# Late modulation in a hybrid diffusion block: w_ada tiles loaded one step ahead, multiplied and added on GpSimd instead of VectorE

## The chip, the cores and the metric

The kernel runs on one core of a Trainium2 chip. The metric is device time in microseconds (us): the median of three runs was 1921.36 us before the change (1921.07 to 1922.86). The engines are named as the profile names them: PE is TensorE's matmuls and PEld its weight loads, DVE is VectorE, ACT is ScalarE, POOL is GpSimd, SP is the engine whose queue issues all the loads.

## The reference

One layer of a block with three parallel token mixers, 256 latent tokens and 256 context tokens of width 2048, all in float32. What is computed, cut to what matters here:

```python
sh_m, sc_m, g_m, sh_f, sc_f, g_f = split(silu(c) @ w_ada + b_ada, 6)   # w_ada: 2048 x 12288
hl = rmsnorm(x) * (1 + sc_m) + sh_m          # and the same for the context
p  = hl @ w_in                               # 2048 x 13376: SSD x, B, C, dt; z; pool; Fourier; gates
y_ssd, y_pool, y_four = ...                  # bidirectional Mamba-2 scan, box pooling, 2-D DFT
merged = g0 * y_pool + g1 * y_four + g2 * y_ssd
x = x + g_m * (merged @ w_out)
x = x + g_f * swiglu(rmsnorm(x) * (1 + sc_f) + sh_f)                    # 2048 -> 5632 -> 2048
return rmsnorm(x) * final_norm_w
```

The first two of the six modulation vectors, `sh_m` and `sc_m`, are needed before the first projection. The other four, 2048 columns of `w_ada` each, are needed later: `sc_f`, `sh_f` and `g_m` around the output projection, `g_f` at the first down projection. These four are the late modulation.

## The kernel before

Every large product is made three times over to keep float32 accuracy: a weight tile `raw` (128 partitions x 1024 numbers, 512 KB) is split into an upper part `whi` by a cast on ACT (`S.copy`, L124) and a lower part `wlo` by a subtraction on DVE (`V.tensor_tensor`, L125), and PE makes upper x upper, lower x upper and upper x lower (`mm3`, L143 to L145). `stage` (L132) does the load and the split; `proj` (L595) goes through a matrix in steps of one `raw` tile, twelve 512-column matmuls for each step. `raw` has four buffers, `whi` and `wlo` three each (pool `wp`).

All loads are issued by one queue, SP. Its order is the order of the program text where the first part is written by hand; behind that, `load` (L95) ties each further load behind the last weight load. So SP issues loads one after another, and each waits until the buffer that it fills has been released. The other engines' order is made by a scheduler from the order of the program text and fixed in the program; each engine works through its own list in that order.

The late modulation is `ada_rest` (L344), a generator. A unit of it is one tile of `w_ada` of 128 rows and 1024 columns: it is loaded into a `raw` buffer, and DVE adds it, times silu(c) of its rows (`sil`, one number per partition), to the accumulator `adacc`: `tensor_scalar` (L353) for the first of sixteen units, `scalar_tensor_tensor` (L355) for the other fifteen. After sixteen units `adacc` is split like a weight, and small matmuls sum over its partitions (`strip` or `ones_r`). There are 8 such sums, 128 units in all. `bg` (L392) makes units behind the steps of the products: the table `BG` says how many units go with each step, 0.5 for the letters x, u, z (and the columns C), 0.35 for p, F, f, q, and 0.45 for s, the first five gate and up products of the SwiGLU. The first 96 units run behind the projections of the mixer; 32 units (`g_f`) run behind the SwiGLU's first products.

In the SSD (`ssd`, L493) ACT and DVE make small matrices `rh` (tag "R", `QR` buffers) that PE turns into decays.

Of the kernel before, what the change touches and what calls it, by code (L numbers as in the profile page):

```python
# [11 lines left out]
F32 = mybir.dt.float32  # L12
F32R = mybir.dt.float32r
AF = mybir.ActivationFunctionType
ALU = mybir.AluOpType

P = 128
D = 2048
KT = D // P
# [17 lines left out]
CH = 512  # L37
# [29 lines left out]

QR, QE = 4, 1
APART, APART2, TURNS0, TURNS1 = 3, 3, 1, 1
ORDER = "u P x0 c x1 u s0 x2 s1 z0 F x3 P z1 s2 p0 F z2 p1 f0 s3 z3 p2 f1 Y f2 p3 q0 f3 q1 q2 q3"  # L70
BG = {"x": 0.5, "z": 0.5, "u": 0.5, "p": 0.35, "F": 0.35, "f": 0.35, "q": 0.35, "s": 0.45}


@with_exitstack
def hybrid_block(ctx: ExitStack, tc, io):
# [24 lines left out]
    def nm(s):  # L100
        names[0] += 1
        return f"{s}{names[0]}"
# [24 lines left out]
    def stage_raw(src, n=CH):  # L127
        raw = wp.tile([P, 2, n], F32, tag="raw", name=nm("raw"), bufs=4)
        last[0] = nc.sync.dma_start(raw, src)
        return raw  # L130
# [15 lines left out]

    # ---------------------------------------------------------------- constants
    pp = C([P, PP_N], nme="pp")
# [40 lines left out]

    # ---------------------------------------------------------------- input norms  # L190
    xnT = [H([P, 2, CH], nme="xnT") for _ in range(8)]
# [37 lines left out]

    # ---------------------------------------------------------------- modulation of the mixer, B and dt  # L230
    Am = C([P, KT, 2], nme="Am")
# [58 lines left out]
    def project_bc(b):  # L290
        """B, dt and the first columns of x of quantum b, in steps"""
        hi, lo = stage(None, CH, w_raw[b][0])
        xhi, xlo = stage(None, 256, w_raw[b][1])
        yield

        def part(out, h, l, cs):
            for k in range(2):
                kt = 2 * b + k
                mm3(out, h[:, k, cs], l[:, k, cs], hh[b][:, k, :], hl[b][:, k, :], kt == 0, kt == KT - 1)

        for ct in range(4):
            part(bacc_[ct], hi, lo, slice(ct * P, (ct + 1) * P))
            yield
        for k in range(2):
            kt = 2 * b + k
            w = dtp[kt // 8][:, kt % 8, :]
            T.matmul(dtps, w, hh[b][:, k, :], start=kt == 0, stop=False)
            T.matmul(dtps, w, hl[b][:, k, :], start=False, stop=kt == KT - 1)
        yield
        for ct in range(2):  # L310
            part(xacc0[ct], xhi, xlo, slice(ct * P, (ct + 1) * P))
            yield
# [4 lines left out]
    nc.sync.dma_start(dtw, rows(w_in, 0, KT, DT_OFF, 64))  # L317
    # the parts of the columns of dt side by side: upper, lower
    dtp = [H([P, 8, P], F32R, nme="dtp") for _ in range(2)]
# [16 lines left out]

    # ---------------------------------------------------------------- background: rest of the modulation
    Af = C([P, KT], nme="Af")
# [4 lines left out]

    def ada_rest(offs):  # L344
        for off in offs:
            for half in range(2):
                a = wp.tile([P, 1024], F32, tag="adacc", name=nm("adacc"), bufs=1)
                for kt in range(KT):
                    raw = wp.tile([P, 1024], F32, tag="raw", name=nm("raw"), bufs=4)
                    c0 = off + half * 1024  # L350
                    load(raw, w_ada[kt * P : (kt + 1) * P, c0 : c0 + 1024])
                    if kt == 0:
                        V.tensor_scalar(a, raw, sil[:, kt : kt + 1], None, ALU.mult)  # L353
                    else:
                        V.scalar_tensor_tensor(a, raw, sil[:, kt : kt + 1], a, ALU.mult, ALU.add)  # L355
                    yield
# [40 lines left out]

    # ---------------------------------------------------------------- convolution
    def conv(dst, src, ct, ns):
        """dst, src: (P, ns, 256); depthwise taps of channel tile ct, then silu."""  # L400
        o = Q([P, ns, 256], nme="cv")
        w = [cwh[:, 5 * ct + k : 5 * ct + k + 1] for k in range(5)]
        S.activation(o, src, AF.Identity, bias=cwh[:, 120 + ct : 121 + ct], scale=w[2])
        for k in (1, 3, 0, 4):
            d = k - 2
            a, b = max(0, -d), 256 - max(0, d)
            V.scalar_tensor_tensor(o[:, :, a:b], src[:, :, a + d : b + d], w[k], o[:, :, a:b], ALU.mult, ALU.add)  # L407
        t = Q([P, ns, 256], nme="cvt")
        S.activation(t, o, AF.Tanh)
        V.scalar_tensor_tensor(dst, t, 1.0, o, ALU.add, ALU.mult)  # L410
# [7 lines left out]

    # ---------------------------------------------------------------- dt, decays
    def cs(ap):  # L420
# [56 lines left out]

    # ---------------------------------------------------------------- B, C
    BT = [H([P, 2, 2, 256], nme="BT") for _ in range(2)]
# [3 lines left out]

    # ---------------------------------------------------------------- SSD
    def bh(ap, n):
# [101 lines left out]

    # ---------------------------------------------------------------- token-major projections
    def h_op(kt, t):
# [154 lines left out]

    # ---------------------------------------------------------------- pooling
    dh, dl = [], []
# [25 lines left out]

    # ---------------------------------------------------------------- Fourier
    tabs = []
# [56 lines left out]

    # ---------------------------------------------------------------- output projection, residual
    def to_feature(chunks, scale=None, colscale=None):
        """(P, 2, CH) token-major chunks to split feature-major (P, 4, 256) tiles."""
        oh, ol = [], []
# [34 lines left out]
    def norm_ffn(t):  # L870
        """scales the rows of token tile t; returns four functions that turn and modulate them"""
        if t == 0:
# [37 lines left out]

    # the last columns and the first of the next product: the norm of one token tile under the products of the other
    def stage_h(w, p, c0):
        raw = wp.tile([P, 2, CH], F32, tag="raw", name=nm("raw"), bufs=4)
        hi, lo = H([P, 2, CH], F32R, nme="hhi"), H([P, 2, CH], F32R, nme="hlo")
        last[0] = nc.sync.dma_start(raw, rows(w, 2 * p, 2, c0, CH))
        split(hi, lo, raw)
        return hi, lo
# [50 lines left out]

    # ---------------------------------------------------------------- SwiGLU
    ah, al = [None] * NFC, [None] * NFC  # L970
# [33 lines left out]

    def down(n0, n1):
        for n in range(4):
            ps = proj(io["w_ffn_down"], 4 * n0, 4 * (n1 - n0), n * CH, pair_op(ah[n0:n1], al[n0:n1]))
            for t in range(2):
                add_down(ps[t], n, t)
# [9 lines left out]
    for n in range(4):  # L1019
        for p in range(2):  # L1020
            raw = wp.tile([P, 2, CH], F32, tag="raw", name=nm("raw"), bufs=4)
            hi, lo = H([P, 2, CH], F32R, nme="dhi"), H([P, 2, CH], F32R, nme="dlo")
# [118 lines left out]
```

## Time and profile before

| | before |
|---|---|
| median of three runs | 1921.36 us (1921.07 to 1922.86) |
| span of the profiled execution | 1922.6 us |
| PE, DVE, ACT, POOL busy | 96%, 64%, 44%, 0% of the span |
| mean granted PE clock | 0.990 |
| bytes moved by DMA | 409.19 MB, mean 213 GB/s |

The profiled execution has no time of its own beside its span, which goes from the first to the last instruction; the span lies inside the range of the three runs, so nothing of weight lies around it. PE's busy share counts a matmul from its start to its modelled end, and these overlap: matmuls of 512 columns start every 0.23 us and are shown as 0.39 us long. A PE that waits shorter than that overlap still reads as busy.

Within the span: the input norms and the early modulation take the first 156 us, the projections of the mixer go to about 1012 us, the output projection to about 1165 us, and then come the SwiGLU's products, of which the first 235 us have the units of `g_f` behind them.

### The profile page before, as it was taken

What the parts mean: (1) busy time and instruction counts of PE and PEld (TensorE: products, weight loads), DVE (VectorE), ACT (ScalarE), POOL (GpSimd) and SP (SyncE); (2) the same over time, 40 slices, a digit from 0 to 9 for tenths busy, and PEclk for the clock granted to TensorE, in tenths of its full rate; (3) what the DMA queues carried; (4) which work ended last, traced back from release to release, by engine and by line L of the source; (5) the groups of instructions that cost most, each with busy time, mean ns of one, the idle gap of its engine ahead of it and who ended that gap; (6) DMA issues with size and microseconds to landing.
All of it is one profiled execution on the core that took longest, in us unless ns stands there. A gap on an engine that the chain in (4) does not pass through costs nothing.

```text
span 1922.6 us, 23276 instructions
## 1 busy us (share of the span) xinstructions
PE 1847.1 (96%) x8804; PEld 1483.4 (77%) x8804; DVE 1236.8 (64%) x1515; ACT 852.5 (44%) x1177; POOL 0.2 (0%) x4
## 2 busy tenths in 40 slices
PE   5999999999999999999999999999999999999998
PEld 3677886867777768777877887787788888888886
DVE  4338869695886687766656657666655555555567
ACT  5225535464464454533434544443343444433444
POOL 0000000000000000000000000000000000000000
PEclk8999999999999999999999999999999999999999
DMA  9985745454656747677777665787766666656655
GB/s 333 353 288 158 243 145 167 142 155 158 186 157 208 248 152 252 216 250 247 244 248 245 201 226 152 256 277 260 247 211 191 196 188 186 191 192 196 187 186 175
DMA packets 214081, 409.19 MB, mean 213 GB/s; under 512 B 14801, under 2 KB 51793, under 8 KB 213969
## 3 DMA queue, kind: packets, MB, share of 16 engines
q1 hardware_dynamic: 213968, 407.71, 67.1%
q8 instruction: 69, 1.13, 0.3%
q14 instruction: 44, 0.35, 0.1%
HBM read 405.56 MB, written 2.10 MB: 212 GB/s over the span
## 4 chain that ended last, share of the span: by engine, by line
PE 66%; DMA 17%; DVE 11%; issue 4%; ACT 2%; DVEq 0%; SPq 0%; ACTq 0%
PE acc L144 19%; PE acc L145 19%; PE acc L143 19%; DMA raw<-w_ada 14%; DVE wlo L125 5%; DVE adacc L355 2%; PE aux L262 1%; DVE cv L407 1%; PE aux L560 1%; DMA t<-ptab 1%; PE aux L522 1%; DMA raw<-w_in 1%; ACT whi L124 1%; PE aux L759 1%; DMA psc<-pool_scale 1%
## 5 line engine op out<-in xcount | busy, mean ns | idle before, releaser
L124 ACT CAST whi<-raw 128x1024 fp32r<-128x1024 f32 (+1 forms) x553 | 574.2, 1040 | 799.5 <-PE acc L145 554.2
L125 DVE TENSOR_TENSOR wlo<-raw,whi 128x1024 fp32r<-128x1024 f32 (+1 forms) x553 | 662.3, 1207 | 354.2 <-ACT whi L124 353.3
L144 PE MATMUL acc<-wlo,h2h 128*128 128x512 f32 x704 | 275.4, 391 | 2.5 <-DVE wlo L125 2.5
L143 PE MATMUL acc<-whi,h2h 128*128 128x512 f32 x704 | 275.0, 391 | 2.3 <-ACT h2h L124 2.3
L145 PE MATMUL acc<-whi,h2l 128*128 128x512 f32 x704 | 275.4, 391 | 0.0
L355 DVE SCALAR_TENSOR_TENSOR adacc<-raw,sil,adacc 128x1024 f32<-128x1024 f32 x120 | 154.0, 1283 | 176.1 <-DMA raw<-w_ada 175.8
L144 PE MATMUL acc<-wlo,lh 128*128 128x512 f32 x512 | 201.8, 394 | 5.4 <-DVE wlo L125 5.4
L143 PE MATMUL acc<-whi,lh 128*128 128x512 f32 x512 | 201.3, 393 | 0.0
L145 PE MATMUL acc<-whi,ll 128*128 128x512 f32 x512 | 200.6, 392 | 0.0
L144 PEld LDWEIGHTS acc<-wlo,h2h 128*128 128x128 f32 x704 | 132.4, 188 | 30.9 <-DVE wlo L125 3.8
L143 PEld LDWEIGHTS acc<-whi,h2h 128*128 128x128 f32 x704 | 132.3, 188 | 29.6 <-ACT h2h L124 2.7
L145 PEld LDWEIGHTS acc<-whi,h2l 128*128 128x128 f32 x704 | 132.5, 188 | 28.2 <-DVE h2l L125 1.3
L145 PE MATMUL acc<-whi,al 128*128 128x512 f32 x320 | 124.7, 390 | 0.0
L144 PE MATMUL acc<-wlo,ah 128*128 128x512 f32 x320 | 124.7, 390 | 0.0
L143 PE MATMUL acc<-whi,ah 128*128 128x512 f32 x320 | 124.6, 389 | 0.0
L144 PEld LDWEIGHTS acc<-wlo,lh 128*128 128x128 f32 x512 | 96.1, 188 | 29.9 <-DVE wlo L125 9.9
L145 PE MATMUL acc<-hh,wlo 128*128 128x512 f32 x288 | 113.8, 396 | 0.8 <-DVE wlo L125 0.8
L144 PE MATMUL acc<-hl,whi 128*128 128x512 f32 x288 | 114.5, 398 | 0.0
L143 PE MATMUL acc<-hh,whi 128*128 128x512 f32 x288 | 112.1, 402 | 0.9 <-ACT whi L124 0.9
L143 PEld LDWEIGHTS acc<-whi,lh 128*128 128x128 f32 x512 | 96.1, 188 | 20.7 <-issue 0.8
L145 PEld LDWEIGHTS acc<-whi,ll 128*128 128x128 f32 x512 | 96.1, 188 | 19.8 <-issue 0.2
L145 PEld LDWEIGHTS acc<-whi,al 128*128 128x128 f32 x320 | 60.1, 188 | 12.4
(294 smaller groups left out, 2467.8 us busy)
## 6 DMA issues: line engine op xcount, KB each, us to landing
raw<-w_in SPq DMA_DIRECT2D x200, 512.0 KB, 4.6
raw<-w_ada SPq DMA_DIRECT2D x192, 512.0 KB, 5.1
raw<-w_ffn_gate SPq DMA_DIRECT2D x88, 512.0 KB, 4.4
raw<-w_ffn_up SPq DMA_DIRECT2D x88, 512.0 KB, 4.4
raw<-w_ffn_down SPq DMA_DIRECT2D x88, 512.0 KB, 4.1
raw<-w_ssd_out SPq DMA_DIRECT2D x32, 512.0 KB, 4.9
raw<-w_out SPq DMA_DIRECT2D x32, 512.0 KB, 4.2
raw<-w_fourier SPq DMA_DIRECT2D x16, 512.0 KB, 4.5
```

The costliest lines, as they stand in the source:

```text
L124: S.copy(hi, src)
L125: V.tensor_tensor(lo, src, hi.bitcast(F32), ALU.subtract)
L143: T.matmul(out, ah, bh, start=first, stop=False)
L144: T.matmul(out, ah, bl, start=False, stop=False)
L145: T.matmul(out, al, bh, start=False, stop=last)
L262: T.matmul(ps[32 * k : 32 * k + 32, o], stat[:, 4 * p + k, :], raws[8 * j + i][:, k, :], start=p == 0, stop=p == 3)
L355: V.scalar_tensor_tensor(a, raw, sil[:, kt : kt + 1], a, ALU.mult, ALU.add)
L407: V.scalar_tensor_tensor(o[:, :, a:b], src[:, :, a + d : b + d], w[k], o[:, :, a:b], ALU.mult, ALU.add)
L522: T.matmul(ps, btk[:, 2 + t, :], xc[d][t], start=t == 0, stop=t == 1)
L560: T.matmul(seg, m, rh, start=n == 0, stop=n == 3)
L759: T.matmul(ps[:, k, :], u_pool[c][:, t, cc_ * P : (cc_ + 1) * P], tb[:, i, t, :], start=t == 0, stop=t == 1)
```

## The change

The units of the late modulation are asked for one unit ahead, in five `raw` buffers instead of four, and are multiplied and added on GpSimd: the first unit of sixteen is one instruction there (`tensor_scalar`), each other unit is two, a `tensor_scalar` in place in `raw` and a `tensor_tensor` that adds it to `adacc`. `QR` goes from 4 to 3, the share of the letter s in `BG` from 0.45 to 0.48, and `down` first uses up what is left of the generator. Lines that only lost a comment are left out, and so are three more places where the tag "raw" now has five buffers.

```diff
-QR, QE = 4, 1
+QR, QE = 3, 1
...
-BG = {"x": 0.5, "z": 0.5, "u": 0.5, "p": 0.35, "F": 0.35, "f": 0.35, "q": 0.35, "s": 0.45}
+BG = {"x": 0.5, "z": 0.5, "u": 0.5, "p": 0.35, "F": 0.35, "f": 0.35, "q": 0.35, "s": 0.48}
...
-        raw = wp.tile([P, 2, n], F32, tag="raw", name=nm("raw"), bufs=4)
+        raw = wp.tile([P, 2, n], F32, tag="raw", name=nm("raw"), bufs=5)
...
     def ada_rest(offs):
+        units = [(off, half, kt) for off in offs for half in range(2) for kt in range(KT)]
+        coming = []
+
+        def ask():
+            off, half, kt = units.pop(0)
+            c0 = off + half * 1024
+            coming.append(wp.tile([P, 1024], F32, tag="raw", name=nm("raw"), bufs=5))
+            load(coming[-1], w_ada[kt * P : (kt + 1) * P, c0 : c0 + 1024])
+
+        ask()
+        yield
         for off in offs:
             for half in range(2):
                 a = wp.tile([P, 1024], F32, tag="adacc", name=nm("adacc"), bufs=1)
                 for kt in range(KT):
-                    raw = wp.tile([P, 1024], F32, tag="raw", name=nm("raw"), bufs=4)
-                    c0 = off + half * 1024
-                    load(raw, w_ada[kt * P : (kt + 1) * P, c0 : c0 + 1024])
+                    if units:
+                        ask()
+                    raw = coming.pop(0)
                     if kt == 0:
-                        V.tensor_scalar(a, raw, sil[:, kt : kt + 1], None, ALU.mult)
+                        nc.gpsimd.tensor_scalar(a, raw, sil[:, kt : kt + 1], None, ALU.mult)
                     else:
-                        V.scalar_tensor_tensor(a, raw, sil[:, kt : kt + 1], a, ALU.mult, ALU.add)
+                        nc.gpsimd.tensor_scalar(raw, raw, sil[:, kt : kt + 1], None, ALU.mult)
+                        nc.gpsimd.tensor_tensor(a, a, raw, ALU.add)
                     yield
...
     def down(n0, n1):
+        for _ in rest:
+            pass
```

VectorE's list, behind a gate of the mixer and its merge (`gt`, `mg`), before the change:

```order
L355 SCALAR_TENSOR_TENSOR adacc_7369<-raw_7490,sil_96,adacc_7369 128x1024
L125 TENSOR_TENSOR wlo_7475<-raw_7472,whi_7474 128x1024
L125 TENSOR_TENSOR wlo_7502<-raw_7499,whi_7501 128x1024
L125 TENSOR_TENSOR wlo_7520<-raw_7517,whi_7519 128x1024
L714 SCALAR_TENSOR_TENSOR gt_7409<-gt_7409,acc_7413 128x512
L714 SCALAR_TENSOR_TENSOR gt_7411<-gt_7411,acc_7414 128x512
L718 TENSOR_TENSOR mg_6916<-mg_6916,gt_7409 128x512
L718 TENSOR_TENSOR mg_6916<-mg_6916,gt_7411 128x512
L125 TENSOR_TENSOR wlo_7538<-raw_7535,whi_7537 128x1024
L355 SCALAR_TENSOR_TENSOR adacc_7369<-raw_7553,sil_96,adacc_7369 128x1024
L125 TENSOR_TENSOR wlo_7559<-raw_7556,whi_7558 128x1024
```

The same place with the change:

```order
L125 TENSOR_TENSOR wlo_7577<-raw_7574,whi_7576 128x1024
L125 TENSOR_TENSOR wlo_7595<-raw_7592,whi_7594 128x1024
L726 SCALAR_TENSOR_TENSOR gt_7465<-gt_7465,acc_7469 128x512
L726 SCALAR_TENSOR_TENSOR gt_7467<-gt_7467,acc_7470 128x512
L730 TENSOR_TENSOR mg_6982<-mg_6982,gt_7465 128x512
L730 TENSOR_TENSOR mg_6982<-mg_6982,gt_7467 128x512
L125 TENSOR_TENSOR wlo_7613<-raw_7610,whi_7612 128x1024
L125 TENSOR_TENSOR wlo_7635<-raw_7632,whi_7634 128x1024
```

Between two lower parts there stood an instruction that waits for a tile of `w_ada`; with the change only weights and the work on products are left in that list.

SP's list, in the second group of x columns (each row a load and what it waits for), before the change:

```order
L97 DMA raw378_2115<-w_ada 128x1024 [waits DMAHW7_49,DVE_49]
L129 DMA raw379_2118<-w_in 128x2x512 [waits DMAHW6_49,DVE_49]
L129 DMA raw382_2148<-w_in 128x2x512 [waits DMAHW0_49,DVE_49]
L97 DMA raw385_2178<-w_ada 128x1024 [waits DMAHW2_49,DVE_49]
L129 DMA raw386_2181<-w_in 128x2x512 [waits DMAHW1_49,DVE_49]
L129 DMA raw389_2211<-w_in 128x2x512 [waits DMAHW3_49,DVE_49]
```

The same place with the change:

```order
L97 DMA raw378_2124<-w_ada 128x1024 [waits Pool_49]
L129 DMA raw379_2128<-w_in 128x2x512 [waits DMAHW5_49,DVE_49]
L129 DMA raw382_2158<-w_in 128x2x512 [waits DMAHW6_49,DMAHW4_49,DVE_49]
L97 DMA raw385_2188<-w_ada 128x1024 [waits Pool_49]
L129 DMA raw386_2192<-w_in 128x2x512 [waits DMAHW0_49,DVE_49]
L129 DMA raw389_2222<-w_in 128x2x512 [waits DMAHW7_49,DMAHW1_49,DVE_49]
```

The loads alternate as before; what a load of `w_ada` waits for here is now GpSimd's release of a buffer, and elsewhere in the list 81 of the weight loads wait for GpSimd too, where they follow a tile of `w_ada` in its buffer.

GpSimd's list, at its start; before the change it held no work of the kernel:

```order
L364 TENSOR_SCALAR adacc265_1454<-raw258_1416,sil13_96 128x1024
L366 TENSOR_SCALAR raw266_1455<-raw266_1455,sil13_96 128x1024
L367 TENSOR_TENSOR adacc265_1454<-adacc265_1454,raw266_1455 128x1024
L366 TENSOR_SCALAR raw273_1494<-raw273_1494,sil13_96 128x1024
L367 TENSOR_TENSOR adacc265_1454<-adacc265_1454,raw273_1494 128x1024
```

More of the change, by code (lines that the diff above doesn't have):

```diff
@@ L912, in stage_h @@
     def stage_h(w, p, c0):
-        raw = wp.tile([P, 2, CH], F32, tag="raw", name=nm("raw"), bufs=4)
+        raw = wp.tile([P, 2, CH], F32, tag="raw", name=nm("raw"), bufs=5)
         hi, lo = H([P, 2, CH], F32R, nme="hhi"), H([P, 2, CH], F32R, nme="hlo")
@@ L1020, in hybrid_block @@
         for p in range(2):
-            raw = wp.tile([P, 2, CH], F32, tag="raw", name=nm("raw"), bufs=4)
+            raw = wp.tile([P, 2, CH], F32, tag="raw", name=nm("raw"), bufs=5)
             hi, lo = H([P, 2, CH], F32R, nme="dhi"), H([P, 2, CH], F32R, nme="dlo")
```

## Prediction

> **What bounds the kernel now.** I read the page's busy table first, then the busy time by stage, then PE's waits, and last one stretch of the timeline.
>
> ```profile
> PE 1847.1 (96%) x8804; PEld 1483.4 (77%) x8804; DVE 1236.8 (64%) x1515; ACT 852.5 (44%) x1177; POOL 0.2 (0%) x4
> ...
> core 0: us, PE busy (x) PEld busy (x) DVE busy (x) ACT busy (x) POOL busy (x), PEclk, DMA share, GB/s
> 156.00:300.00 144.00, 137.87 (x706) 116.26 (x705) 118.41 (x153) 64.26 (x92) 0.00 (x0) 0.98 0.61 184
> ...
> 700.00:800.00 100.00, 97.92 (x479) 78.57 (x478) 80.02 (x116) 60.61 (x106) 0.00 (x0) 1.00 0.64 203
> 800.00:900.00 100.00, 94.63 (x410) 76.06 (x409) 60.41 (x57) 39.08 (x41) 0.00 (x0) 1.00 0.74 247
> 900.00:1012.00 112.00, 108.53 (x473) 88.01 (x473) 70.97 (x67) 45.31 (x46) 0.00 (x0) 1.00 0.76 249
> ...
> 1210.00:1362.00 152.00, 143.45 (x638) 116.78 (x637) 102.81 (x97) 61.56 (x65) 0.00 (x0) 0.99 0.80 264
> ...
> 1500.00:1700.00 200.00, 200.00 (x899) 165.17 (x898) 105.24 (x100) 84.85 (x89) 0.00 (x0) 1.00 0.65 190
> ```
>
> PE bounds it. From 1500 to 1700 us the SwiGLU runs without late modulation, and PE is busy all the time. From 1210 to 1362 us the same products have the units behind them, and PE is idle for 152.00 - 143.45 = 8.55 us; from 800 to 1012 us, with units again, for 5.37 + 3.47 us. So what there is to win lies in such idle time, and it is small. Who ends it, from 600 to 1420 us:
>
> ```profile
> PE acc L144 <- DVE wlo L125: 14.0, 16, 1.7
> PE aux L992 <- DVE sg L985: 6.0, 4, 3.0
> PE aux L522 <- DVE xc L516: 2.5, 1, 2.5
> PE acc L143 <- ACT h2h L124: 2.3, 1, 2.3
> ...
> DVE adacc L355 <- DMA raw<-w_ada: 136.7, 60, 4.9
> ```
>
> PE waits for DVE, 14.0 us for lower parts of weights and 6.0 us for the SwiGLU's products. DVE, though not full, has stood 136.7 us waiting for tiles of `w_ada` in this stretch. One such place (DVE, SP, ACT and PE rows):
>
> ```profile
> 822.04 2.35 DVE L125 TENSOR_TENSOR wlo<-raw,whi 128x1024 fp32r<-128x1024 f32 x2
> ...
> 824.42 0.34 SPq L97 DMA_DIRECT2D raw<-w_ada  x1
> ...
> 826.71 1.22 DVE L125 TENSOR_TENSOR wlo<-raw,whi 128x1024 fp32r<-128x1024 f32 x1
> 829.75 1.28 DVE L355 SCALAR_TENSOR_TENSOR adacc<-raw,sil,adacc 128x1024 f32<-128x1024 f32 x1 [1.81 <-DMA raw<-w_ada]
> 830.95 3.49 DVE L125 TENSOR_TENSOR wlo<-raw,whi 128x1024 fp32r<-128x1024 f32 x3
> ...
> 826.17 1.06 ACT L124 CAST whi<-raw 128x1024 fp32r<-128x1024 f32 x1 [1.69 <-PE acc L145]
> 828.89 1.05 ACT L124 CAST whi<-raw 128x1024 fp32r<-128x1024 f32 x1 [1.66 <-PE acc L145]
> ...
> 832.22 0.50 PE L144 MATMUL acc<-wlo,lh 128*128 128x512 f32 x1 [0.42 <-DVE wlo L125]
> ```
>
> A `wlo` ends at 824.4 us and frees a buffer; only then SP can load the next `w_ada` tile, which lands some 5 us later. DVE gets to it at 827.9, stands for 1.81 us, spends 1.28 us, and the lower part behind it comes too late: PE stops. The casts are 828.89 - 826.17 = 2.72 us apart; that is PE's pace, one step of twelve matmuls.
>
> **The change part by part.** *DVE loses the units.* What it spends on them:
>
> ```profile
> L355 DVE SCALAR_TENSOR_TENSOR adacc<-raw,sil,adacc x120: 1269/1284/1287, 151.8 to 1390.4; 128x1024 f32<-128x1024 f32 x120
> L353 DVE TENSOR_SCALAR adacc<-raw,sil x8: 747/753/755, 145.2 to 1293.7; 128x1024 f32<-128x1024 f32 x8
> ...
> raw<-w_in SPq DMA_DIRECT2D x200, 512.0 KB, 4.6
> raw<-w_ada SPq DMA_DIRECT2D x192, 512.0 KB, 5.1
> ```
>
> 120 x 1.284 + 8 x 0.753 = 160 us of DVE time go, and with them every wait for `w_ada` on that engine. PE's part of this is at most the 14.0 + 6.0 us above. The stage without units shows that nothing is left of either wait when units are absent, so I count all of it: -20.0 us. The 2.5 us for `xc` come from the SSD's own chain and are not counted.
>
> *GpSimd gains 120 pairs and 8 single instructions.* The trace has no such operation. From below, a pair costs no less than DVE's nearest: 0.753 us for one scalar and one tensor, 1.22 us (the `wlo` rows) for two tensors, 1.97 us together. From above, GpSimd would become the bound when a pair takes longer than the distance of two units: in the stages with 0.5 of a unit per step that is 2.72 / 0.5 = 5.44 us, with 0.48 it is 5.67 us. I take 3.5 us, between the ends and nearer to the row of the only engine that does such work. Up to 5.44 us it lies beside PE's products and costs nothing. The Trainium skill's "GPSIMD Engine Reference", section 3.1, gives 4497 ns for an addition of two float32 tensors of 2048 numbers per partition; half of it, and about 0.85 us for a one-input pass at the line rate that section 4.1 speaks of, make an estimate of 3.1 us, with which nothing in this sum would change. No run here shows it.
>
> *One more buffer, one unit ahead.* SP waits for buffers in turn, so a buffer comes round every fourth load before, every fifth after. With 1.5 loads per step that is 4 x 2.72 / 1.5 = 7.25 us before and 9.07 us after. A weight needs 4.6 us to land, about 1.05 for its cast and 1.22 for its lower part, 6.9 us; a `w_ada` tile needed 5.1 + 1.28 = 6.4 us and whatever DVE was late, and will need 5.1 + 3.5 = 8.6 us. Three rounds, of which one holds a `w_ada` tile, need 6.9 + 6.9 + 6.4 = 20.2 of 21.8 us before and 22.4 of 27.2 us after. So the longer hold is paid for by the fifth buffer; the loads behind a late `w_ada` tile on SP are weights, with the upper and lower parts of two further steps, 5.4 us, ready before PE runs dry. Price: nothing; if the cover were gone, each microsecond over is one on PE.
>
> *Three `rh` buffers instead of four.* ACT has waited for PE there five times already:
>
> ```profile
> ACT rh L557 <- PE aux L560: 20.6, 5, 6.1
> ```
>
> One more such wait is 20.6 / 5 = 4.1 us on ACT, which delays the casts queued behind it; they stand two steps ahead. Between 0 and 4.1 us; I take 1.
>
> *0.48 instead of 0.45, and the rest used up in `down`.* The five first gate and up products have 72 steps with units: 34.6 calls, where 32 units, the first asking and the end need 34. So nothing is left for `down`. The DMA share of 0.80 there rises by 1.48 / 1.45 to 0.82. Nothing. The products that sum `adacc` over partitions come later in PE's list by a unit, which is the cover for GpSimd's last pair. Nothing.
>
> *The beginning, 156 to 300 us*, has DVE at 118.41 of 144.00 us already, and it is where GpSimd and DVE would meet most. The next part prices that at 14.9 us if they exclude each other and at nothing if not; I leave 2 us in the sum, near the lower end, since nothing in the trace shows two engines excluding each other.
>
> Sum: -20.0 + 0 + 0 + 1 + 0 + 2 = -17 us. The profiled execution's span is 1922.6 us and lies within the three runs, so it stands for them: 1921.4 - 17 = 1904 us.
>
> **The rivals.** *GpSimd and DVE take turns at SBUF (slower).* If an instruction of the one holds back the other's, the time of both adds up. DVE's share for the units, `wlo` of `adacc` included (one split of 1.23 us where ACT's column counts one):
>
> ```profile
> core 0: us, DVE busy (x) ACT busy (x), PEclk, DMA share, GB/s
> 156.00:300.00 144.00, 23.74 (x19) 1.06 (x1) 0.98 0.61 184
> ...
> 700.00:800.00 100.00, 12.99 (x11) 1.05 (x1) 1.00 0.64 203
> ...
> 900.00:1012.00 112.00, 18.68 (x15) 1.05 (x1) 1.00 0.76 249
> ...
> 1210.00:1362.00 152.00, 30.23 (x24) 1.05 (x1) 0.99 0.80 264
> ```
>
> From 156 to 300 us DVE keeps 118.41 - 22.5 = 95.9 us, 18 units at 3.5 us add 63.0: 158.9 us of work in 144.0, 14.9 us too much. From 700 to 800 us 80.02 - 11.8 + 35.0 = 103.2 us, 3.2 too much; from 1210 to 1362 us 102.81 - 29.0 + 80.5 = 154.3 us, 2.3 too much. From 900 to 1012 us there is room: 70.97 - 17.5 + 49.0 = 102.5 of 112. The full stages keep PE's old idle time and add 20.4 us; two further hundreds of the SSD, as full as that from 700, add about 2; the stretch from 800 to 1012 us still loses its waits, some 9 us (all of PE's idle time there). 1921.4 + 22 - 9 = 1934 us. It decides from the pair at which the first stage is full, (144.0 - 95.9) / 18 = 2.7 us. For it: DVE is the engine with the least room there, and lower parts delayed by a whole GpSimd instruction reach PE at once. Against it: DVE's wait for `w_ada` cost it up to 4.9 us at a time, and PE mostly rode that out. The Trainium skill says in "SBUF — State Buffer", section "Who interferes with whom", that a DVE instruction with two SBUF inputs and a GpSimd instruction that reads SBUF share one read port and that the second to issue is fully blocked; `wlo<-raw,whi` is such an instruction. By that rule this rival is what happens; the trace, with POOL idle, can neither confirm nor deny it.
>
> *The waits only change hands (no change).* PE's idle time after 156 us has other roots too: the SSD's chain, tables that are loaded late. If what DVE gains is used up by PE waiting a little later for those, or GpSimd's release holds SP as DVE's did, the time stays: 1921 us, within 0.2%. For it: DVE's busy share is 64%, so it isn't short of time but of order. Against it: from 1210 to 1362 us there is no SSD, and PE's waits there vanish as soon as the units do.
>
> *The pair is longer than the units' distance (slower).* At 6.5 us, 1.06 us over 5.44 and 0.83 over 5.67: some 32 units in the stages with 0.5 and 34 behind the SwiGLU give 34 + 28 = 62 us, 1983 us. For it: two instructions for one, in software. Against it: 6.5 us is over three times DVE's time.
>
> **How the numbers follow.** The forecast, 1904 us, gets 0.50; taking turns, 1934 us, 0.27; no change, 1921 us, 0.13; the long pair, 0.10. The forecast's own range is 1891 to 1916 us: at best 13 us more go, from the waits of the beginning and of `xc`, at worst three fifths of the 20 us stay. A time of 0.2% (3.8 us) off is about what a measurement of this kernel can tell from no change. Faster gets 0.52 (the forecast, and a little of the middle case), no change 0.12, slower 0.36. The range leaves out the long pair and little else: 1890 to 1948 us, upwards 14 us over the second case's point, for a pair of 4 us in the first stage, a loss of 23.9 us in place of 14.9, and some wear elsewhere.
>
> **What would show it.** After the change DVE's list must have no wait for `w_ada`, and DVE must be busy for about 1077 us. Right: PE's wait L144 for `wlo` falls from 14.0 us to a few, `sg` from 6.0 to nearly none, and PE's idle time behind the SwiGLU from 8.55 us to 2 or less. Taking turns shows in the length of the `wlo` rows: over 1.22 us in the mean with units, unchanged from 1500 us on; GpSimd's own rows would spread too. The long pair shows as SP waiting for POOL. What would make the forecast wrong is above all a mean `wlo` beyond 1.8 us in the first 300 us.

## The result, and the profile after

The changed kernel takes 2265.14 us (median of four runs, 2262.28 to 2267.8) where the kernel before takes 1921.21 us: a ratio of 1.1769, 95% interval 1.1738 to 1.18. The forecast was 1904 us with a range up to 1948 us; the time came out 317 us above the range and on the other side of no change.

The busy table of the changed kernel, its two main GpSimd groups (line, engine, operation, tiles, count, then busy time, mean ns of one, idle time before and what ended most of it), and one row of the loads:

```profile
PE 1966.1 (87%) x8804; PEld 1540.5 (68%) x8804; DVE 1268.4 (56%) x1387; ACT 850.8 (38%) x1177; POOL 749.4 (33%) x252
...
L366 POOL TENSOR_SCALAR raw<-raw,sil 128x1024 f32<-128x1024 f32 x120 | 391.1, 3259 | 659.2 <-DMA raw<-w_ada 397.1
L367 POOL TENSOR_TENSOR adacc<-adacc,raw 128x1024 f32<-128x1024 f32 x120 | 334.4, 2787 | 9.9
...
raw<-w_ada SPq DMA_DIRECT2D x192, 512.0 KB, 4.9
```

GpSimd is busy for only a third of the span and stands 397.1 us waiting for tiles of `w_ada`, yet everything has become slower. A pair takes 3.26 + 2.79 = 6.05 us. Who holds the loads, in SP's waits (total us, times, longest):

```profile
SPq L129 <- POOL adacc L367: 661.8, 78, 12.2
SPq L129 <- DVE wlo L125: 627.5, 289, 24.4
SPq L97 <- POOL adacc L367: 345.8, 42, 10.6
...
SPq L129 <- POOL adacc L364: 20.7, 3, 9.1
SPq L97 <- POOL adacc L364: 17.8, 4, 5.1
```

SP waits 661.8 + 345.8 = 1007.6 us for GpSimd's additions. L97 is a load of `w_ada`; L129 is a load of a weight, and 78 of those stood behind a unit as well. With the first units of sixteen (L364) 127 loads wait for GpSimd, as good as one for each of the 128 units. Before, SP waited in the same way for the units on DVE, but for 114.4 + 46.2 = 160.6 us:

```profile
SPq L129 <- DVE adacc L355: 114.4, 82, 4.1
...
SPq L97 <- DVE adacc L355: 46.2, 32, 5.0
```

The loads that come late are felt on the other engines:

```profile
ACT whi L124 <- DMA raw<-w_in: 294.8, 87, 10.3
...
PE acc L143 <- ACT whi L124: 80.1, 43, 4.6
PE acc L144 <- DVE wlo L125: 79.4, 75, 11.8
```

By stage (columns as in the windows shown before):

```profile
core 0: us, PE busy (x) PEld busy (x) DVE busy (x) ACT busy (x) POOL busy (x), PEclk, DMA share, GB/s
...
1500.00:1700.00 200.00, 158.68 (x580) 120.79 (x580) 95.18 (x67) 55.33 (x59) 128.21 (x44) 0.87 0.53 181
1900.00:2100.00 200.00, 200.00 (x896) 165.33 (x895) 107.87 (x106) 81.84 (x83) 0.00 (x0) 1.00 0.63 191
```

From 1900 us on, with no units left, PE makes 896 matmuls in 200 us, as before (899). With units behind the SwiGLU it makes 580, is idle for 41 us of the 200, and its granted clock is 0.87 instead of 1.00. One stretch there (SP's and GpSimd's rows of the timeline) shows the mechanism:

```profile
1562.52 0.34 SPq L97 DMA_DIRECT2D raw<-w_ada  x1
1562.95 0.90 SPq L129 DMA_DIRECT2D raw<-w_ffn_gate  x2
1572.22 0.34 SPq L97 DMA_DIRECT2D raw<-w_ada  x1
1572.67 0.88 SPq L129 DMA_DIRECT2D raw<-w_ffn_up  x2
1581.96 0.34 SPq L97 DMA_DIRECT2D raw<-w_ada  x1
...
1566.37 2.85 POOL L366 TENSOR_SCALAR raw<-raw,sil 128x1024 f32<-128x1024 f32 x1 [3.88 <-DMA raw<-w_ada]
1569.30 2.89 POOL L367 TENSOR_TENSOR adacc<-adacc,raw 128x1024 f32<-128x1024 f32 x1
1576.12 2.85 POOL L366 TENSOR_SCALAR raw<-raw,sil 128x1024 f32<-128x1024 f32 x1 [3.92 <-DMA raw<-w_ada]
1579.05 2.88 POOL L367 TENSOR_TENSOR adacc<-adacc,raw 128x1024 f32<-128x1024 f32 x1
```

SP issues a tile of `w_ada` at 1562.52. It lands at about 1566.4, GpSimd multiplies and adds it until 1572.19, and 0.03 us later SP issues the next tile of `w_ada`, and behind it two weights. That load was meant to be one unit ahead, but it goes into the buffer that GpSimd was just reading. Since SP works in order, the weights behind it wait too: two weights get through in 9.7 us, where PE needs 5.44 us for them. The buffer addresses in the two compiled programs say how often that is so. Of 128 units, 44 have their buffer taken by the very next load of `w_ada`, and 63 by a weight one to three loads later. Before, these were 37 and 79, so the assignment is no new one; only the hold was shorter then.

The size fits. The first multiplication starts at 152.5 us and the last addition ends at 1722 us; less one pause of 154 us without units that makes 1415 us for 127 units, 11.1 us each, against 4.9 + 6.05 = 10.95 us for landing and pair. Before, the last unit ended at 1392 us. So 330 of the 338 us between the two spans lie ahead of the last unit.

### The profile page after: what moved, and what is told of

It is laid out like the page before. It is cut to its first block, busy times and chain, and to the rows that moved or that the text cites. A ratio compares the mean times of both kernels' runs of the same rounds, so it can differ in the third digit from the quotient of the medians.

```text
span 2260.5 us, 23410 instructions
## 1 busy us (share of the span) xinstructions
PE 1966.1 (87%) x8804; PEld 1540.5 (68%) x8804; DVE 1268.4 (56%) x1387; ACT 850.8 (38%) x1177; POOL 749.4 (33%) x252
## 5 line engine op out<-in xcount | busy, mean ns | idle before, releaser
L125 DVE TENSOR_TENSOR wlo<-raw,whi 128x1024 fp32r<-128x1024 f32 (+1 forms) x553 | 770.0, 1397 | 741.9 <-ACT whi L124 736.2
L366 POOL TENSOR_SCALAR raw<-raw,sil 128x1024 f32<-128x1024 f32 x120 | 391.1, 3259 | 659.2 <-DMA raw<-w_ada 397.1
L367 POOL TENSOR_TENSOR adacc<-adacc,raw 128x1024 f32<-128x1024 f32 x120 | 334.4, 2787 | 9.9
L143 PE MATMUL acc<-whi,h2h 128*128 128x512 f32 x704 | 287.2, 408 | 30.0 <-ACT whi L124 27.6
L144 PE MATMUL acc<-wlo,h2h 128*128 128x512 f32 x704 | 288.4, 410 | 16.4 <-DVE wlo L125 16.3
L145 PE MATMUL acc<-whi,h2l 128*128 128x512 f32 x704 | 286.1, 406 | 0.0
L144 PE MATMUL acc<-wlo,lh 128*128 128x512 f32 x512 | 217.7, 425 | 52.0 <-DVE wlo L125 51.8
L143 PE MATMUL acc<-whi,lh 128*128 128x512 f32 x512 | 214.2, 419 | 32.9 <-ACT whi L124 31.7
L145 PE MATMUL acc<-whi,ll 128*128 128x512 f32 x512 | 211.6, 413 | 0.0
L364 POOL TENSOR_SCALAR adacc<-raw,sil 128x1024 f32<-128x1024 f32 x8 | 23.9, 2989 | 303.4 <-DMA raw<-w_ada 292.5
L143 PE MATMUL acc<-hh,whi 128*128 128x512 f32 x288 | 114.4, 409 | 6.1 <-ACT cin L697 3.4
```

Of the source, the lines that this page charges most:

```text
L125: V.tensor_tensor(lo, src, hi.bitcast(F32), ALU.subtract)
L143: T.matmul(out, ah, bh, start=first, stop=False)
L144: T.matmul(out, ah, bl, start=False, stop=False)
L145: T.matmul(out, al, bh, start=False, stop=last)
L364: nc.gpsimd.tensor_scalar(a, raw, sil[:, kt : kt + 1], None, ALU.mult)
L366: nc.gpsimd.tensor_scalar(raw, raw, sil[:, kt : kt + 1], None, ALU.mult)
```

## The experiments

Two theories stood against each other. **The loop** (Theory A in the expectations): a buffer filled with `w_ada` is given to the next loads, so SP stands through landing and pair. **Taking turns** (Theory B): GpSimd and DVE hold each other up at SBUF. The length of the pair by itself came in as a third. What was expected of each run stands ahead of its result.

Each ratio is to the kernel before in the same set of runs. Its median was 1921.21 to 1927.5 us from set to set, so a difference in us between runs of two sets can be off by some 6 us.

### Only the engine, and all but the engine

The kernel before with nothing changed but the engine:

```diff
-                        V.scalar_tensor_tensor(a, raw, sil[:, kt : kt + 1], a, ALU.mult, ALU.add)
+                        nc.gpsimd.tensor_scalar(raw, raw, sil[:, kt : kt + 1], None, ALU.mult)
+                        nc.gpsimd.tensor_tensor(a, a, raw, ALU.add)
```

> The kernel before with only the engine changed: pairs on GpSimd, four raw buffers, nothing asked ahead, four rh buffers, 0.45. Theory A: the same loop with a buffer less for the weights, 2260 to 2400 us. Theory B: the same instructions meet as in the changed kernel, 2230 to 2300 us. If the five buffers and the asking ahead had helped as the prediction said, it is slower than the changed kernel by 20 us or more; if they do nothing, the same.

Measured: 2284.37 us, ratio 1.1869 (1.1814 to 1.1924). SP's waits in it:

```profile
SPq L129 <- POOL adacc L356: 644.1, 75, 11.7
...
SPq L97 <- POOL adacc L356: 385.9, 45, 10.9
```

Four buffers or five, ahead or not, SP waits about as long for GpSimd, 1030 us here. This run is 19 us slower than the changed kernel, just under the 20 us named as the sign that buffers and asking ahead help; so they help little. The other half, the changed kernel with the units back on VectorE:

```diff
-                        nc.gpsimd.tensor_scalar(raw, raw, sil[:, kt : kt + 1], None, ALU.mult)
-                        nc.gpsimd.tensor_tensor(a, a, raw, ALU.add)
+                        V.scalar_tensor_tensor(a, raw, sil[:, kt : kt + 1], a, ALU.mult, ALU.add)
```

> The changed kernel with the units back on VectorE (one instruction each, as before); five buffers, one unit ahead, three rh buffers and 0.48 stay. Theory A, the buffer loop: in the changed kernel a load stands on SP until GpSimd gives back the buffer of a tile of w_ada that was loaded just before it, and landing (4.9 us) and pair (6.05 us) follow one another, 11 us where two units are 5.4 to 7.8 us apart. Here the hold is 5.1 + 1.28 = 6.4 us again: 1905 to 1925 us. Theory B, turns: GpSimd's instructions hold up VectorE's at SBUF; no GpSimd here, so 1900 to 1925 us too. If instead the asking ahead, the rh buffers or 0.48 are the cause, it stays above 1950 us.

Measured: 1932.8 us, ratio 1.0037 (1.0016 to 1.0058), so slightly slower than before and 8 us above what either theory gave, far from the 344 us of the change. DVE's and PE's waits in it:

```profile
DVE adacc L366 <- DMA raw<-w_ada: 160.8, 68, 5.0
...
PE acc L144 <- DVE wlo L125: 26.9, 22, 5.3
```

The same wait in the whole of the profile before:

```profile
DVE adacc L355 <- DMA raw<-w_ada: 175.8, 82, 4.9
```

Asking a unit ahead takes 15 of 175.8 us from DVE's wait for `w_ada`. The load is written earlier in the program, but it is not made earlier. The loss comes with the engine, and the fifth buffer and the asking ahead take back at most those 19 us of it.

### Taking the loop away

The tiles of `w_ada` get two buffers of their own out of the five, and the weights keep three:

```diff
-            coming.append(wp.tile([P, 1024], F32, tag="raw", name=nm("raw"), bufs=5))
+            coming.append(wp.tile([P, 1024], F32, tag="ada", name=nm("ada"), bufs=2))
...
-        raw = wp.tile([P, 2, n], F32, tag="raw", name=nm("raw"), bufs=5)
+        raw = wp.tile([P, 2, n], F32, tag="raw", name=nm("raw"), bufs=3)
```

> The changed kernel, its pairs on GpSimd, but the late tiles of w_ada have two buffers of their own and the weights three, the same memory. A load of w_ada then waits for the pair two units back, and no weight load waits for GpSimd. Theory A: landing and pair overlap, what is left is the pair itself (6.05 us beside 5.4 to 7.8): 1930 to 2010 us. Theory B: the same GpSimd and VectorE instructions run beside each other: 2200 us or more.

Measured: 1977.97 us, ratio 1.0277 (1.0226 to 1.0328), as the loop expected and not taking turns. Its groups, and SP's wait for GpSimd:

```profile
L366 POOL TENSOR_SCALAR ada<-ada,sil 128x1024 f32<-128x1024 f32 x120 | 431.4, 3595 | 334.4 <-DMA ada<-w_ada 334.2
L367 POOL TENSOR_TENSOR adacc<-adacc,ada 128x1024 f32<-128x1024 f32 x120 | 310.3, 2586 | 10.0
L125 DVE TENSOR_TENSOR wlo<-raw,whi 128x1024 fp32r<-128x1024 f32 x537 | 758.6, 1419 | 501.8 <-ACT whi L124 500.9
...
SPq L97 <- POOL adacc L367: 102.6, 34, 4.8
```

The pair is as long as in the change (6.18 us), and so is `wlo`; only the buffers differ, and 287 us are gone. SP's wait for the pairs' additions falls from 1007.6 to 102.6 us. So the loop carries most of the loss, and neither the length of the pair nor `wlo` can be its main cause. The check with the loop put back, one own buffer instead of two and four for the weights (`bufs=1` and `bufs=4` in the diff above):

> As the run with own buffers, but one for w_ada and four for the weights: no weight ever waits for a buffer from GpSimd, yet every load of w_ada waits for the pair just before it, and SP, in order, keeps the weights behind it. Theory A (a unit costs its landing and its pair, one after the other): 128 units of 4.9 + 6.05 = 11 us make 1400 us in place of the 1090 us that the units' stages took before, 2200 to 2280 us. If what hurts is that weights take over buffers that GpSimd holds, 1980 us or less. Theory B (turns at SBUF): the same instructions as in that run, 1980 us.

Measured: 2201.97 us, ratio 1.1449 (1.1401 to 1.1497), at the lower end of what the loop gives and far from the 1980 us of the two other answers.

```profile
SPq L97 <- POOL adacc L367: 850.4, 110, 15.2
```

Now 110 loads of `w_ada` wait for the pair of the tile before it, and no load of a weight waits for GpSimd. The 63 us from here to the changed kernel are not taken apart further. The third test shortens the hold. The multiplication is left out, so the sums lack `silu(c)`:

```diff
-                        nc.gpsimd.tensor_scalar(raw, raw, sil[:, kt : kt + 1], None, ALU.mult)
```

> The changed kernel without the multiplication: each unit but the first of sixteen is GpSimd's addition alone, so the modulation comes out wrong; everything else stays. Theory A: a unit is 4.9 + 2.6 = 7.5 us, which fits the stages of 0.35 (7.8 us a unit) and is 2 us too long where units are 5.4 to 5.7 us apart: 1940 to 2030 us. Theory B: GpSimd meets VectorE half as long, about half of the loss is left, 2060 to 2120 us.

Measured: 2028.23 us, ratio 1.0546 (1.0507 to 1.0584), at the upper end of what the loop gave and below what taking turns gave.

```profile
SPq L129 <- POOL adacc L366: 279.5, 98, 5.7
```

An instruction of 3.26 us less for each unit saves 237 us, though GpSimd was idle two thirds of the time. Three runs, one that takes the loop away, one that puts it back and one that shortens it, came out as the loop says.

### What is left without the loop

The run with own buffers is still 53 us above the kernel before in its set (1925.22 us). The same with the units on VectorE:

> As the first, units on VectorE, with two buffers of their own for w_ada and three for the weights. Theory A: VectorE's waits for w_ada (175.8 us before) fall below 40 us, and PE's waits for wlo with them: 1895 to 1915 us. If three buffers are too few for the weights, 1925 to 1960 us. Theory B says nothing of it.

Measured: 1907.37 us, ratio 0.9907 (0.9872 to 0.9942). It is 0.9% below the kernel before, and 25 us below the same kernel without own buffers (1932.8 us). VectorE's and PE's waits in it:

```profile
DVE adacc L366 <- DMA ada<-w_ada: 97.1, 70, 4.0
...
PE acc L144 <- DVE wlo L125: 4.8, 8, 1.4
```

With a buffer of its own the load does come earlier. DVE's wait is not under 40 us as expected, but PE's wait for `wlo` is nearly gone: the gain that the forecast sought from the engine came from the buffers. From here to the GpSimd form it is 1977.97 - 1907.37 = 71 us. Next, GpSimd does half as much: the multiplication is left out and own buffers are kept:

> The same without the multiplication (the modulation comes out wrong), with two buffers for w_ada and three for the weights. What the run with own buffers still lost against the same buffers on VectorE, some 70 us, is either GpSimd's length (5.2 us alone, 6.2 us as measured, against units 5.4 us apart) or turns with VectorE. If it is the length, 2.4 us is far below the distance: 1905 to 1920 us. If it is turns, the addition, which reads two tensors, keeps about half: 1935 to 1955 us.

Measured: 1945.02 us, ratio 1.0113 (1.0079 to 1.0147), as taking turns expected: 38 us for the additions alone, 33 us more for the multiplications. SP's wait for the additions is down from 102.6 to 5.2 us in it, so the 38 us are hardly the length of GpSimd's work; whether the 33 us are, this run doesn't say. To see the accesses without any wait for GpSimd, the kernel before was given GpSimd pairs on a tile that nobody else uses. A one-column copy on DVE (`mark`) starts each pair, and `QR` is 3 to make room:

```diff
                         V.scalar_tensor_tensor(a, raw, sil[:, kt : kt + 1], a, ALU.mult, ALU.add)
+                        m = wp.tile([P, 1], F32, tag="mark", name=nm("mark"), bufs=4)
+                        V.tensor_copy(m, a[:, 0:1])
+                        nc.gpsimd.tensor_scalar(dmy, dmy, m, None, ALU.mult)
+                        nc.gpsimd.tensor_tensor(dmy, dmy, dmy, ALU.add)
```

> The kernel before, with its units on VectorE, and beside each of them but the first of sixteen a pair of the same size on GpSimd, in a tile of its own that nobody waits for (three rh buffers; VectorE copies one column per unit as a mark to start the pair). No load depends on GpSimd. Theory A: nothing of the loop is here, 1921 to 1945 us (marks and turns). Theory B: the instructions meet as in the changed kernel, and VectorE has its units besides: 2200 us or more. The mean wlo, 1.22 us without GpSimd, shows the turns: 1.4 us or more if they are real.

Measured: 2036.27 us, ratio 1.0583 (1.0558 to 1.0608). Neither number was met; 115 us were more than the loop theory allowed to accesses and far less than the 344 us of the change. The mean `wlo` is 1.35 us, above the 1.22 us without GpSimd, though not the 1.4 us named. The run to compare it with has marks without pairs (the last two lines of the diff left out):

> The kernel before with the one-column mark copies on VectorE, three R buffers and the idle tile of the run with pairs beside, but without GpSimd's pairs. That run took 2036.27 us, 115 us over the kernel before. If GpSimd's pairs cost those 115 us, this one takes 1920 to 1940 us, and SP's waits for wlo stay near the 869.9 us of before. If the marks, the R buffers or another order of the work cost them, it takes 1990 us or more.

Measured: 1952.68 us, ratio 1.0142 (1.0091 to 1.0193), between the two answers. So 84 us belong to the pairs, and 25 us (against 1927.5 us for the kernel before in its set) to something in the preparation. The same two runs with own buffers on VectorE (two R buffers, and the pair as two halves of 512 columns, to make room), first without pairs:

> The same without GpSimd's instructions: marks, two R buffers and the idle tile alone, the measure for the run with pairs. Both theories: 1903 to 1922 us, wlo near 1.23 us. If it takes over 1940 us, marks or R buffers cost time, and the run with pairs is to be compared with this one and not with 1907 us.

Measured: 1932.37 us, ratio 1.0042 (1.0015 to 1.0068), 10 us above the range that both theories gave and again 25 us over the run without marks. Then with pairs:

> The kernel with the units on VectorE and two buffers of their own for w_ada (1907.37 us), to which each unit adds a mark copy and, on GpSimd, two multiplications and two additions over 512 columns of a tile that nobody else uses, so as many numbers as the pair of the change; two R buffers instead of three. GpSimd holds no load buffer here, so no load can wait for it. Theory that the 71 us between the GpSimd and the VectorE form with own buffers are SBUF accesses beside GpSimd: 1955 to 2000 us, wlo near 1.4 us. Theory that those 71 us are the longer hold of a w_ada buffer: 1905 to 1925 us here, whatever wlo's mean is.

Measured: 2011.05 us, ratio 1.0455 (1.0405 to 1.0504), which is above both ranges, but 79 us over the run without pairs. In all runs with four marks PE does less in a stretch in which neither units nor marks run. The first row is the run with marks alone, then with own buffers and marks, then with own buffers and pairs:

```profile
1500.00:1700.00 200.00, 200.00 (x878) 1.00 0.63 186
```

```profile
1500.00:1700.00 200.00, 200.00 (x878) 161.78 (x877) 102.97 (x99) 82.11 (x86) 0.00 (x0) 1.00 0.63 186
```

```profile
1500.00:1700.00 200.00, 200.00 (x870) 161.22 (x869) 103.41 (x100) 79.89 (x81) 0.00 (x0) 1.00 0.62 187
```

PE is busy all the time at a granted clock of 1.00 and makes 870 to 878 matmuls instead of 899. PE does the same kind of work there. What differs is that the tiles that PE loads as stationary operands (`h2h`, `h2l`, `ah`, `al`), with the rest of their pool, lie 128 bytes further, behind four marks of 32 bytes. The last run puts them back by doubling the marks:

```diff
-                        m = wp.tile([P, 1], F32, tag="mark", name=nm("mark"), bufs=4)
+                        m = wp.tile([P, 1], F32, tag="mark", name=nm("mark"), bufs=8)
```

> The run with pairs beside and own buffers (2011.05 us) with eight mark tiles instead of four, and nothing else. The mark tiles take 32 bytes per partition each, and the tiles of the pool that holds PE's weights (h2h, h2l, ah, al) lie right behind them. In the runs with marks these started at an address of 64 beyond a multiple of 256, in all other runs at 192, and there PE made 870 to 878 matmuls in the full 200 us from 1500 to 1700 us, where the kernel before made 899. Eight marks bring the tiles back to 192. Theory that the place of the tiles cost PE those 2.4%, and the marks nothing: 895 to 900 matmuls in these 200 us, and 1975 to 1995 us in all, so that GpSimd's pairs alone cost 68 to 88 us over the 1907.37 us without them. Theory that the marks' instructions or the R buffers did it: 870 to 878 matmuls again, and 2003 to 2020 us.

Measured: 1986.7 us, ratio 1.0331 (1.0299 to 1.0362), as the place of the tiles expected. Its rows (window, group, wait):

```profile
1500.00:1700.00 200.00, 200.00 (x895) 165.36 (x894) 107.32 (x103) 82.50 (x85) 0.00 (x0) 1.00 0.64 191
```

```profile
L125 DVE TENSOR_TENSOR wlo<-raw,whi 128x1024 fp32r<-128x1024 f32 x537 | 716.1, 1341 | 342.8 <-ACT whi L124 342.0
```

```profile
ACT whi L124 <- DMA raw<-w_in: 152.8, 75, 6.3
```

PE is back at 895, and the pairs cost 1986.7 - 1907.37 = 79 us, with no load waiting for GpSimd at all. The mean `wlo` is 1.34 us, against 1.22 us in the run without pairs and marks. So GpSimd's work beside VectorE's is enough to account for the 71 us, without any wait for a buffer that GpSimd holds. How it reaches the end, the last row suggests: ACT waits 152.8 us for `w_in`, and in the run without pairs and marks:

```profile
ACT whi L124 <- DMA raw<-w_in: 90.0, 47, 6.7
```

A longer `wlo` gives its `raw` buffer back later, and the load behind it starts later; this reading fits the rows but no run isolates it. The 79 us are rather a high value: `QR` 2 and the marks' 18 us of DVE time were not taken out, and the four halves keep GpSimd busy for 7.1 us a unit instead of 6.2.

## Why the prediction was wrong

The 344 us can be laid out in one order: 2265.14 - 1977.97 = 287 us for the loop, 71 us for GpSimd's work beside VectorE, and 1907.37 - 1921.21 = -14 us for what own buffers give on VectorE (-18 us against the kernel before in its own set). The parts are not independent. At its shortest the pair takes 5.18 us, in the loop 6.05 us in the mean; if accesses are what lengthens it, they make the loop longer too, by 0.87 us of 11.1 for each unit.

**One more buffer, one unit ahead: "nothing". This step failed, and it decided.** It assumed that buffers come round in turn, every fifth load. They don't: 44 + 63 = 107 of 128 tiles of `w_ada` hand their buffer to the next load of `w_ada` or to a weight at most three loads later. With that, the hold of 8.6 us that this same step worked out is no share of three rounds in 27.2 us but a wait of the whole queue; SP stood 1007.6 us in such waits, and a unit took 11.1 us. The addresses, or which unit a load's wait on GpSimd refers to, would have shown it; both loads of `w_ada` in the rows of SP's list shown with the change already wait for GpSimd, and so do the 81 weight loads counted beside them. With the step's own numbers, 8.6 us a unit against 5.44 and 5.67 us in the full stages, the 32 and 34 units there would cost 101 + 100 = some 200 us, an estimate.

**The pair of 3.5 us was too short.** Its rows in the changed kernel (minimum, median, maximum in ns):

```profile
L366 POOL TENSOR_SCALAR raw<-raw,sil x120: 2844/2922/5496, 152.5 to 1716.2; 128x1024 f32<-128x1024 f32 x120
...
L367 POOL TENSOR_TENSOR adacc<-adacc,raw x120: 2339/2818/4912, 155.4 to 1719.2; 128x1024 f32<-128x1024 f32 x120
```

At least 2.84 + 2.34 = 5.18 us, 6.05 in the mean, just inside and beyond the bound of 5.44 us at which the prediction let a pair cost something. The addition is what the Trainium skill's "GPSIMD Engine Reference", section 3.1, gives for it, by an estimate (half of 4497 ns, 2.25 us). The multiplication is not: the near line rate for one input that section 4.1 speaks of made an estimate of 0.85 us of it, and it takes longer than the addition. Here the measurement decides. Own buffers hide most of even such a pair, so this error alone would not have made 344 us.

**-20.0 us from PE's waits.** The sign named for it came true by half: DVE's list has no wait for `w_ada` any more. But PE's wait for `wlo` rose from 16.3 us over the whole span to 79.4 us, because weights came late. That these waits can go was right; own buffers on VectorE took PE's wait for `wlo` down to 4.8 us, and the whole down by 14 to 18 us.

**Nothing for 0.48, `QR` and `down`; 2 us for the beginning.** The run with the units back on VectorE bounds all these edits together, and asking ahead, at 0.4% slower (1932.8 against 1925.22 us). They were next to no part of the loss. The beginning cost far more than 2 us; PE was busy for 137.87 of the 144.00 us with 706 matmuls, and is now for 115.92 with 549:

```profile
156.00:300.00 144.00, 115.92 (x549) 96.81 (x548) 108.91 (x110) 48.03 (x73) 81.38 (x27) 0.88 0.42 139
```

**The rival of taking turns** had its mechanism right and its size wrong. `wlo` has a mean of 1.41 us with the change, against 1.22 before:

```profile
L125 DVE TENSOR_TENSOR wlo<-raw,whi 128x1024 fp32r<-128x1024 f32 x537 | 757.4, 1414 | 740.2 <-ACT whi L124 734.4 <-PE aux L377 2.0 <-PE aux L520 0.4
...
L125 DVE TENSOR_TENSOR wlo<-raw,whi x553: 677/1226/3457, 39.5 to 2223.5; 128x1024 fp32r<-128x1024 f32 x179, 128x512 fp32r<-128x512 f32 x6
...
L125 DVE TENSOR_TENSOR wlo<-raw,whi x164: 1215/1226/1227, 1749.4 to 2199.5; 128x1024 fp32r<-128x1024 f32 x164
```

The second row is the whole span (minimum, median, maximum), the third the stretch from 1750 us on, where no unit runs: no `wlo` is over 1.23 us there, while with units single ones reach 3.46 us. From 156 to 300 us the mean of the 128 x 1024 tiles is 1.42 us, so the sign that was to tell above all of a wrong forecast, 1.8 us there, did not come, and the forecast was wrong for another reason. DVE is busy for 1268.4 us instead of the 1077 us named, 191 us more in lengthened instructions, while ACT's 850.8 us are unchanged (852.5). That agrees with the Trainium skill's "SBUF — State Buffer", section "Who interferes with whom": DVE's two-input instructions and GpSimd's reads exclude each other, and ACT waits for no one. But the rival charged only the stretches in which both times no longer fit, 22 us. Measured are 71 to 84 us, perhaps since a stretched `wlo` also keeps its load buffer. That alone would have made the kernel before some 1992 to 2005 us, an estimate, and not 2265.

**The long pair** came nearest: SP did wait for POOL, as its sign said. Its price of 62 us counted the distance of units that was overrun, and not the landing of a load that cannot start before the pair ends. Missing from the rivals was the one that happened, that asking ahead doesn't take place because the buffer isn't free.

## What to carry to other kernels

A load written earlier is only made earlier if the buffer that it gets is free earlier: look up which tile held the buffer before, and count landing and consumer as one hold of an in-order queue. Give a stream with another consumer its own buffers (at least two) before moving it to another engine; here that alone was worth 287 us on the slow engine, and on the fast one the kernel came out 0.9% below the one before. One buffer of its own was not enough (2201.97 us). Idle time of the consumer does not show that it has room, since a consumer inside such a loop is idle while it is the cause.

## What the runs showed of the hardware that was not expected

- A GpSimd multiplication by one number per partition (2.84 us for 128 x 1024 float32) takes longer than the addition of two tensors (2.34 us); both are the shortest in the changed kernel.
- PE's rate hung on where its stationary tiles lie, with the rest of their pool. At an address of 64 beyond a multiple of 256 bytes it made 870 to 878 matmuls in 200 us, at 192 beyond 895 to 899, at a granted clock of 1.00 both times; with the move by 128 bytes back, the whole kernel took 24 us less (2011.05 to 1986.7). Only these two places were tried, and the tiles of moving operands (`whi`, `wlo`) lay at 192 in all these runs, so the rule behind it stays open.
- Where PE stands often, its granted clock is lower as well: 0.87 from 1500 to 1700 us with the change and a mean of 0.937 over the span, against 0.990 before.

Open is why the buffers are handed on in this order, and whether more than two own buffers would give more; neither was tried. Open too is how much of the 25 us of preparation is the place of the tiles, since with the tiles put back only the run with pairs was made.
